# One step of a hybrid DeltaNet and attention backbone: the first norm with all shift and scale columns on TensorE, and smaller background pieces in DeltaNet

## The chip, the cores and the metric

The kernel runs on one core of a Trainium2 chip. The metric is the device time of one execution in microseconds, the median of several. TensorE does matrix products into PSUM, VectorE and ScalarE work element by element, GpSimd can do a few of VectorE's operations and cannot read PSUM, and SyncE (SP) issues all transfers between memory and the on-chip buffers. Each engine works through its own queue in order; semaphores hold an instruction back until its inputs are there.

## The reference

128 context tokens and 512 latent tokens, 640 together, go through one layer of width 2048. Everything is fp32.

```python
def ada_modulation(cond, w_ada, b_ada):
    m = jax.nn.silu(cond) @ w_ada + b_ada          # (B, 6 * D)
    return jnp.split(m[:, None, :], N_MOD, axis=-1)
...
    shift1, scale1, gate1, shift2, scale2, gate2 = ada_modulation(cond, p['w_ada'], p['b_ada'])
    h = modulate(rms_norm(x, p['norm1_g']), shift1, scale1)      # h * (1 + scale) + shift
    qkv, z, a, b, q_a, kv_a, k_pe = split_cols(h @ p['w_in'], IN_SPLITS)
    gdn_o, s_fin = gdn_mix(qkv, z, a, b, ...)      # silu(conv(qkv)), l2 norm, delta rule both ways, 8 heads
    ...                                            # 8 heads of latent attention, w_out, gated residual
    x = x + gate2 * conv_ffn(h2, p['w_up'], p['ffn_conv_w'], p['ffn_conv_b'], p['w_down'])
```

Context and latent tokens have a conditioning vector each (`c_ctx`, `c`), so every modulation column is made for two vectors. In DeltaNet each chunk needs the inverse of a unit triangular matrix.

## The kernel before, in words

**Number format.** A weight tile W is split into `whi`, a rounded copy in the type fp32r (ScalarE, line 129), and `wlo` = W - `whi` (VectorE, line 131). A dense product is then three fp32r products: whi·hi, whi·lo, wlo·hi. Activations carry the same split (`h_hi`, `h_lo`). Products in plain fp32 also occur, for small things; the profile shows each of them as two records.

**Dense products.** w_in is stored so that its columns come as z0 to z4, misc, then k, q, v of each head in turn, with the low-rank columns m and the last z between. `dense` (line 212 on) makes a pair of 128-column tiles from four weight chunks `kg`, each a load of 512 KB: 4 x 2 x 3 x 8 = 192 products of 320 columns. `w_next` keeps two raw chunks, and split chunks, ahead. Every 12 products `tick` advances the background generators, among them one per DeltaNet head.

**The first norm (lines 356 to 438).** x (16 tiles of 128 rows, `xs`) is loaded, squared on ScalarE and summed on VectorE (line 381, two buffers `sq`); `col_sums` puts the sum over rows on TensorE (line 244), and `rb` becomes 1/rms by Ln and Exp. The modulation columns come in units of 256. `ada` loads a unit's weights in four chunks of 512 KB (`araw`, a ring of three), splits each, and multiplies with the conditioning vectors as the four stationary columns (lines 264, 265: 32 products of 256 columns). ScalarE copies the 4 x 256 result out of PSUM (line 267), two small products turn it (line 272), VectorE adds the bias and the gain. `modulated` then makes v = x · scale · rb in four VectorE operations per unit (line 287), `h_hi` on ScalarE (line 289) and `h_lo` (line 290), for odd tiles on GpSimd. `part` does all that for one unit after the other. Eight units belong to scale1; with two of them done a quarter of the contraction of the first three tiles z0, z1, z2 can run. Six further units give 1536 of the 2048 shift columns beside the pair z3, z4. The last 512 shift columns come from `gemv_fill`, a background job on VectorE (line 326). The shift enters the later dense products as two extra columns of `h_hi` and `h_lo`.

**DeltaNet.** For each head, `sink` runs the convolution and the SiLU as soon as the dense tile is there, and spawns `gdn` and `gdn_q`. `gdn` solves the triangular blocks of both directions in one batch; one direction needs its blocks turned, which is a copy on ScalarE of 20 rows x 1024 with the two inner axes exchanged, on the way in (line 629) and on the way out (line 647). `neg` is minus the decay factor, for all heads at once. A `yield n` gives the engines to the dense stream for n ticks.

**Attention entry.** `kv_cache` and `key_rope` load the cached latents and rotary keys at the place in the program where they are split.

The order of the instructions on each engine is the order of a scheduler that goes by priorities from the program's order, so it is not exactly the order in the text.

Of the kernel before, what the change touches and what calls it, by code (L numbers as in the profile page):

```python
# [15 lines left out]
P = 128  # L16
# [29 lines left out]
NSP = 6  # L46
LA = 1
# [3 lines left out]
PK = ()  # L51
SH = 1.0
# [15 lines left out]
def step_kernel(ctx: ExitStack, tc: tile.TileContext, a, dbg=None, stop=None):  # L68
# [183 lines left out]
    def ada_load(c, kg, pl):  # L252
        raw = pl.tile([P, 4, 256], F32, tag="wraw", name="araw", bufs=3)
        sp.dma_start(raw, a["w_ada"][c, kg])
        return raw

    def ada(n, t0, cond, pl):

        ps = bank("ada_ps")
        for kg in range(4):  # L260
            hi, lo = split_chunk(ada_load(n, kg, pl), 256, pl, 3, (4 * n + kg) % 8 in PK)
            for k in range(4):
                kt = kg * 4 + k
                pe.matmul(ps[0:4, 0:256], cond[:, kt, :], hi[:, k, :], start=kt == 0, stop=False)
                pe.matmul(ps[0:4, 0:256], cond[:, kt, :], lo[:, k, :], start=False, stop=kt == 15)
# [3 lines left out]
        def last():  # L269
            ps2 = bank("ada_ps2")  # L270
            for j in range(2):
                pe.matmul(ps2[:, 2 * j:2 * j + 2], m4[:, j * P:(j + 1) * P], con[0:4, K_COMB:K_COMB + 2],
                          start=True, stop=True)
            dve.tensor_tensor(mod[:, t0:t0 + 2, :], ps2[:, 0:4].rearrange("p (j c) -> p j c", c=2),
                              v1(V_BADA + t0, 2).unsqueeze(2).broadcast_to([P, 2, 2]), ALU.add)
# [83 lines left out]
    h_hi = hp.tile([P, KT, T + 2], F32R, name="h_hi")  # L359
    h_lo = hp.tile([P, KT, T + 2], F32R, name="h_lo")  # L360
    zb = hp.tile([P, EZ, 2], F32, name="zb")

    def hmov(kt):
        return h_hi[:, kt, :], h_lo[:, kt, :]

    fill["ps"] = lambda: bank("ada_ps")
    with tc.tile_pool(name="xp", bufs=1, side="right") as xp:
        cond = xp.tile([P, KT, 4], F32R, name="cond")
        dve.tensor_copy(cond[:, :, 0:2], csil)
        dve.tensor_tensor(cond[:, :, 2:4], csil, cond.bitcast(F32)[:, :, 0:2], ALU.subtract)  # L370
        xs = xp.tile([P, KT, T], F32, name="xs")
        for c in range(8):
            sp.dma_start(xs[:, 2 * c:2 * c + 2, :], a["x"][:, 2 * c:2 * c + 2, :])
        acc = xp.tile([P, T], F32, name="acc1")
        for kt in range(KT):
            if kt == 0:
                act.activation(acc, xs[:, 0, :], AF.Square)
            else:
                sq = xp.tile([P, T], F32, tag="sq", name="sq", bufs=2)
                act.activation(sq, xs[:, kt, :], AF.Square)  # L380
                dve.tensor_tensor(acc, acc, sq, ALU.add)
        rb = xp.tile([P, T], F32, name="rb1")
        rstd_bcast(rb, col_sums(acc), 1.0 / D)

        def part(j):
            if j < 8:
                ada(j, 16 + 2 * j, cond, xp)()
                gain(16 + 2 * j, V_N1 + 2 * j, 2)
                for kt in (2 * j, 2 * j + 1):
                    v = xp.tile([P, T], F32, tag="sq", name="v", bufs=2)  # L390
                    modulated(xs, rb, h_hi, h_lo, kt, 16, v)

        def early(i, ps):

            zr = xp.tile([P, T], F32, tag="sq", name="zr", bufs=2)
# [22 lines left out]
        fill["step"] = SH  # L418
        fill["gen"] = gemv_fill([xp, 2, 1], ada_jobs(2 * NSP, 16))
        todo = list(range(NSP))  # L420
        last = []
        npair = (EZ - 3) // 2
        for p in range(1, 1 + npair):
            def shift(kg):
                n = 4 * (p - 1) + kg + 1
                while todo and (NSP - len(todo)) * 4 * npair < n * NSP:
                    c = todo.pop(0)
                    f = ada(8 + c, 2 * c, cond, xp)
                    if last:
                        last.pop()()  # L430
                    last.append(f)
                if last and n == 4 * npair:
                    last.pop()()
            dense(hmov, lambda i, ps: early(1 + 2 * p + i, ps), before=shift)
        for _ in fill["gen"]:
            pass
        dve.tensor_copy(h_hi[:, :, T:T + 2], mod[:, 0:KT, :])
        dve.tensor_tensor(h_lo[:, :, T:T + 2], mod[:, 0:KT, :], h_hi.bitcast(F32)[:, :, T:T + 2], ALU.subtract)
# [55 lines left out]
    neg = gp.tile([P, 5, 16], F32, name="neg")  # L494
# [3 lines left out]
    def gates(ps):  # L498
# [43 lines left out]
        dve.tensor_scalar(neg, eg, -1.0, None, ALU.mult)  # L542
# [4 lines left out]
    def gdn(h, st):  # L547
# [12 lines left out]
        gm = gmask(0)  # L560

# [19 lines left out]
        cc = gp.tile([P, 3, 2, 5], F32, name="cc", bufs=2)  # L581
        for d in range(2):
            dve.tensor_tensor(cc[:, 0, d, :], beta[:, :, 8 * d + h], rec, ALU.mult)
            dve.tensor_scalar(cc[:, 1, d, :], cc[:, 0, d, :], -1.0, None, ALU.mult)
            dve.tensor_tensor(cc[:, 2, d, :], cc[:, 0, d, :], edec[:, :, 8 * d + h], ALU.mult)

# [1355 lines left out]
```

## Time and profile before

| what | us |
|---|---|
| median of three runs | 3266.69 (3266.14 to 3268.99) |
| the profiled execution | 3265.16 |
| its span in the trace | 3263.4 |
| x being loaded and squared | 0 to 24 |
| tiles z0, z1, z2 with the first norm | 24 to 147 |
| tiles z3, z4 with the shift units | 147 to 206 |
| DeltaNet beside the other w_in columns | 206 to 990 |
| entry of the attention | 990 to 1045 |
| attention, w_out, FFN, last norm | 1045 to 3263 |

The stages are read from the first and last instructions of their lines. The span is the time between the first and the last instruction; 1.8 us of the execution lie around it. In the windows a busy time is a sum over the stretch, and PEclk is the share of full speed that TensorE was granted. In the waits a line says which instruction waited, for which engine's write to which tile, how long in all, how often, and the longest.

### The profile page before, as it was taken

The numbers are of one execution on the slowest core, as the hardware profiler recorded it, in microseconds if no ns is written. First come the engines' busy times: TensorE is split into PE (matmuls) and PEld (weight loads), VectorE is DVE, ScalarE is ACT, GpSimd is POOL, SyncE is SP. The second block draws the span as 40 slices with busy tenths as digits, with TensorE's granted clock in tenths as the row PEclk, the third lists the DMA queues.
The fourth block names the chain that finished last, engine by engine and source line by source line (L and its number), as shares of the span: only waits on it lengthen the run. The fifth ranks groups of instructions, "written<-read, shape, count | busy, mean of one in ns | idle before, by whom it ended". The sixth has DMA issues, their size and how long they took to land. (4 is left out here: it accounts for less than half of the span.)

```text
span 3263.4 us, 54513 instructions
## 1 busy us (share of the span) xinstructions
PE 3071.6 (94%) x21243; PEld 2972.8 (91%) x21243; DVE 2684.3 (82%) x4701; ACT 1453.0 (45%) x2245; POOL 334.3 (10%) x279
## 2 busy tenths in 40 slices
PE   5899999999998998997899999999999989999996
PEld 4689999999998998997899999999999989999995
DVE  7666666767567677998998898898898898999998
ACT  5434555555446543114544444444444454444433
POOL 1201000000000000003200000000010041111111
PEclk9899999999899999998999999999999999999998
DMA  7663222323224126883343333343343332333333
GB/s 271 201 198 86 72 78 67 117 68 100 74 87 135 45 81 236 270 263 121 127 136 97 110 128 108 111 131 110 98 140 102 95 125 94 113 98 110 110 116 121
DMA packets 181474, 403.92 MB, mean 124 GB/s; under 512 B 39392, under 2 KB 57952, under 8 KB 181216
## 3 DMA queue, kind: packets, MB, share of 16 engines
q1 hardware_dynamic: 181216, 400.44, 38.3%
q8 instruction: 167, 2.74, 0.4%
q14 instruction: 91, 0.75, 0.1%
HBM read 361.83 MB, written 38.54 MB: 123 GB/s over the span
## 5 line engine op out<-in xcount | busy, mean ns | idle before, releaser
L922 ACT CAST whi<-wraw 128x1024 fp32r<-128x1024 f32 x256 | 268.8, 1050 | 489.4 <-PE dn L198 202.8
L198 PE MATMUL mm<-b_hi,whi 128*128 128x320 f32 x1344 | 398.6, 310 | 4.2 <-ACT whi L922 3.9
L198 PE MATMUL mm<-b_lo,whi 128*128 128x320 f32 x1344 | 397.8, 310 | 0.0
L923 DVE TENSOR_TENSOR wlo<-wraw,whi 128x1024 fp32r<-128x1024 f32 x256 | 318.0, 1242 | 71.9 <-PE dn L207 62.9
L326 DVE SCALAR_TENSOR_TENSOR aacc<-araw,csil,aacc 128x512 f32<-128x512 f32 x510 | 369.0, 762 | 9.1 <-DMA araw<-in_w_ada_dram 8.7
L198 PE MATMUL mm<-h_lo,whi 128*128 128x320 f32 (+1 forms) x1312 | 318.7, 321 | 17.5 <-POOL h_lo L290 17.5
L198 PE MATMUL mm<-h_hi,whi 128*128 128x320 f32 (+1 forms) x1312 | 324.2, 327 | 7.5 <-ACT h_hi L289 4.8
L198 PE MATMUL dn<-b_hi,whi 128*128 128x320 f32 x1008 | 297.7, 309 | 0.0
L198 PE MATMUL dn<-b_lo,whi 128*128 128x320 f32 x1008 | 297.7, 309 | 0.0
L129 ACT CAST whi<-wraw 128x1024 fp32r<-128x1024 f32 (+1 forms) x138 | 143.0, 1036 | 327.3 <-PE mm L198 227.1
L198 PEld LDWEIGHTS mm<-b_hi,whi 128*128 128x128 f32 x1344 | 253.2, 188 | 5.0 <-ACT whi L922 4.4
L198 PEld LDWEIGHTS mm<-b_lo,whi 128*128 128x128 f32 x1344 | 253.2, 188 | 0.0
L198 PEld LDWEIGHTS mm<-h_lo,whi 128*128 128x128 f32 x1312 | 227.3, 194 | 21.5 <-POOL h_lo L290 19.6
L198 PEld LDWEIGHTS mm<-h_hi,whi 128*128 128x128 f32 x1312 | 227.2, 195 | 13.0 <-ACT h_hi L289 6.8
L1593 PE MATMUL mm<-b_hi,whi 128*128 128x320 f32 x672 | 204.6, 318 | 33.1 <-DVE x_lo L1600 9.4
L207 PE MATMUL mm<-h_hi,wlo 128*128 128x320 f32 (+1 forms) x1312 | 234.1, 318 | 0.0
L922 ACT CAST whi<-us 128x1024 fp32r<-128x1024 f32 (+1 forms) x126 | 123.4, 980 | 230.7 <-PE mm L198 160.3
L207 PE MATMUL mm<-b_hi,wlo 128*128 128x320 f32 x1344 | 224.4, 309 | 0.0
L131 DVE TENSOR_TENSOR wlo<-wraw,whi 128x1024 fp32r<-128x1024 f32 (+1 forms) x138 | 168.2, 1219 | 54.2 <-ACT whi L129 23.7
L207 PEld LDWEIGHTS mm<-h_hi,wlo 128*128 128x128 f32 x1312 | 202.8, 192 | 1.6
L207 PEld LDWEIGHTS mm<-b_hi,wlo 128*128 128x128 f32 x1344 | 204.0, 188 | 0.0
L1593 PE MATMUL mm<-b_lo,whi 128*128 128x320 f32 x672 | 202.2, 314 | 0.0
(534 smaller groups left out, 7461.2 us busy)
## 6 DMA issues: line engine op xcount, KB each, us to landing
wraw<-in_w_up_dram SPq DMA_DIRECT2D x176, 512.0 KB
araw<-in_w_ada_dram SPq DMA_DIRECT2D x272, 256.0 KB
wraw<-in_w_down_dram SPq DMA_DIRECT2D x88, 512.0 KB
wraw<-in_w_in_dram SPq DMA_DIRECT2D x80, 512.0 KB
araw<-in_w_ada_dram SPq DMA_DIRECT2D x56, 512.0 KB
wraw<-in_w_out_dram SPq DMA_DIRECT2D x32, 512.0 KB
graw<-g_d SPq DMA_DIRECT2D x44, 320.0 KB
g_d<-cg SPq DMA_DIRECT2D x44, 256.0 KB
```

The costliest lines, as they stand in the source:

```text
L129: act.copy(hi[:, :, 0:n], raw[:, :, 0:n])
L131: (pool if on_pool else dve).tensor_tensor(lo[:, :, 0:n], raw[:, :, 0:n], hi.bitcast(F32)[:, :, 0:n], ALU.subtract)
L198: pe.matmul(o, wts[0][:, k, col:col + P], m[:, sl], start=start and k + n == 0, stop=False)
L207: pe.matmul(o, wts[1][:, k, col:col + P], mov(k)[0][:, sl], start=False, stop=stop and k == 3)
L326: dve.scalar_tensor_tensor(acc[:, c, 0:w], raw, vecs[:, kt, c:c + 1], acc[:, c, 0:w], ALU.mult, ALU.add)
L922: act.copy(dst_hi, src)
L923: dve.tensor_tensor(dst_lo, src, dst_hi.bitcast(F32), ALU.subtract)
L1593: pe.matmul(dq[q], wt(w[0], k), bs[(2 * n + k) % 6][m][:, q, :], start=n == grp[0] and k + m == 0, stop=False)
```

## The change

First norm. The tiles of x now lie in the buffers that `h_hi` takes over later, two tiles to a buffer; with the room that this gives, the raw ring has eight chunks and the split buffers five. Every second square goes to TensorE as it is and is summed there. All 16 units of scale1 and shift1 go through `ada`; for the first eight the first chunk is multiplied unsplit in plain fp32. A unit's turn and all that follows is issued after the next unit's products. `h_lo` is always VectorE's. DeltaNet. The turning copies are cut in two with a step between. The SiLU of k, q and v moves from `sink` into the first step of a background generator. There is one more step before a head's last turn, and minus the decay factor is made per head. Attention entry. The cache loads are issued before the first projection.

```diff
-NSP = 6
-LA = 1
+NSP = 8
+AR = 8
+AH = 5
...
     def ada(n, t0, cond, pl):
         ps = bank("ada_ps")
         for kg in range(4):
-            hi, lo = split_chunk(ada_load(n, kg, pl), 256, pl, 3, (4 * n + kg) % 8 in PK)
+            raw = pl.tile([P, 4, 256], F32, tag="wraw", name="araw", bufs=AR)
+            sp.dma_start(raw, a["w_ada"][n, kg])
+            whole = n < 8 and kg == 0
+            movs = ((1, raw),) if whole else [(0, w) for w in split_chunk(raw, 256, pl, AH)]
             for k in range(4):
                 kt = kg * 4 + k
-                pe.matmul(ps[0:4, 0:256], cond[:, kt, :], hi[:, k, :], start=kt == 0, stop=False)
-                pe.matmul(ps[0:4, 0:256], cond[:, kt, :], lo[:, k, :], start=False, stop=kt == 15)
+                for m, (c, w) in enumerate(movs):
+                    pe.matmul(ps[0:4, 0:256], cond[c][:, kt, :], w[:, k, :], start=kt + m == 0,
+                              stop=kt == 15 and m == 1)
...
+            sq = acc if kt == 0 else xp.tile([P, T], F32, tag="sq", name="sq", bufs=4)
+            act.activation(sq, xs[kt // 2][:, kt % 2, 0:T], AF.Square)
+            if kt % 2:
+                for o, sl in tok_chunks(sums):
+                    pe.matmul(o, ones, sq[:, sl], start=kt == 1, stop=False)
+            elif kt:
                 dve.tensor_tensor(acc, acc, sq, ALU.add)
...
+        def ada_last():
+            if last:
+                n, f = last.pop()
+                f()
+                if n < 8:
+                    gain(16 + 2 * n, V_N1 + 2 * n, 2)
...
+                    for k, v in enumerate(vs_):
+                        act.copy(h_hi[n][:, k, 0:T], v)
+                        dve.tensor_tensor(h_lo[n][:, k, 0:T], v, h_hi[n].bitcast(F32)[:, k, 0:T], ALU.subtract)
...
+        def ada_next(count):
+            for _ in range(count):
...
+                f = ada(n, 16 + 2 * n if n < 8 else 2 * n - 16, (cond, condf), xp)
+                ada_last()
+                last.append((n, f))
...
-            for j in range(LA) if kg == 0 else ():
-                part(j)
-            for j in (2 * kg, 2 * kg + 1):
-                part(j + LA)
+            if kg == 0:
+                ada_next(1)
+                w_load(0)
+                w_load(1)
+            ada_next(3 if kg == 0 else 2)
...
-        fill["gen"] = gemv_fill([xp, 2, 1], ada_jobs(2 * NSP, 16))
...
-        act.copy(L[0:20], Lc[0:20].rearrange("p a b -> p b a"))
-        yield 1
+        for i in range(2):
+            act.copy(L[0:20, 16 * i:16 * i + 16, :], Lc[0:20, :, 16 * i:16 * i + 16].rearrange("p a b -> p b a"))
+            yield 1
...
+    def gdn_v(st, v):
+        act.activation(v, v, AF.Silu)
+        st["v"] = v
+        yield 1
...
             conv(ps, V_CW + off, 24, dst)
-            act.activation(dst, dst, AF.Silu)
```

In TensorE's queue, at the start of the second quarter of the contraction, before: `mm0`, `mm1`, `mm2` are the tiles z0 to z2, `ada_ps` the unit under way, and the dense products use the two tiles of x that the unit before it has just made:

```order
L265 MATMUL ada_ps_480<-wlo_499,cond_96 4x256
L264 MATMUL ada_ps_480<-whi_511,cond_96 4x256
L198 MATMUL mm0_161<-h_hi_90,whi_450 128x320 x2
L198 MATMUL mm1_162<-h_hi_90,whi_450 128x320 x2
L198 MATMUL mm2_163<-h_hi_90,whi_628 128x320 x2
L198 MATMUL mm0_161<-h_lo_91,whi_450 128x320 x2
L198 MATMUL mm1_162<-h_lo_91,whi_450 128x320 x2
L198 MATMUL mm2_163<-h_lo_91,whi_628 128x320
L198 MATMUL mm0_161<-h_hi_90,whi_450 128x320 x2
L198 MATMUL mm1_162<-h_hi_90,whi_450 128x320
L265 MATMUL ada_ps_480<-wlo_513,cond_96 4x256
```

and in the changed kernel, where `h_hi2`, `h_lo2` come from unit 2, and the two lines L271 are the turns of units 3 and 4:

```order
L271 MATMUL ada_ps_369<-con_73,m4_418 128x2 x2
L198 MATMUL mm0_177<-h_hi2_430,whi_496 128x320 x2
L198 MATMUL mm0_177<-h_lo2_431,whi_496 128x320
L271 MATMUL ada_ps_526<-con_73,m4_575 128x2 x2
L198 MATMUL mm0_177<-h_lo2_431,whi_496 128x320
L198 MATMUL mm0_177<-h_hi2_430,whi_496 128x320 x2
L198 MATMUL mm0_177<-h_lo2_431,whi_496 128x320
L264 MATMUL ada_ps_593<-araw_594,condf_103 4x256 x4
L264 MATMUL ada_ps_593<-whi_602,cond_102 4x256
L264 MATMUL ada_ps_593<-wlo_604,cond_102 4x256
L264 MATMUL ada_ps_593<-whi_602,cond_102 4x256
```

The dense products stood among the products of one unit, taking tile by tile; now the turns of units 3 and 4 stand close together, and all products of unit 5 lie between them and the first use of what unit 3 makes.

In VectorE's queue, for the first unit's two tiles, there is one difference `h_lo` before, the other being GpSimd's; `aacc` is the background job of shift columns:

```order
L274 TENSOR_TENSOR mod_78<-ada_ps2_223,vec_72 128x4
L131 TENSOR_TENSOR wlo_396<-wraw_392,whi_394 128x4x128
L282 SCALAR_TENSOR_TENSOR mod_78<-mod_78,vec_72 128x4
L287 SCALAR_TENSOR_TENSOR v_228<-xs_99,mod_78,rb1_155 128x512
L287 SCALAR_TENSOR_TENSOR v_228<-xs_99,mod_78,rb1_155 128x128
L287 SCALAR_TENSOR_TENSOR v_233<-xs_99,mod_78,rb1_155 128x512
L287 SCALAR_TENSOR_TENSOR v_233<-xs_99,mod_78,rb1_155 128x128
L131 TENSOR_TENSOR wlo_271<-araw_267,whi_269 128x1024
L290 TENSOR_TENSOR h_lo_91<-v_228,h_hi_90 128x640
L131 TENSOR_TENSOR wlo_285<-araw_281,whi_283 128x1024
L131 TENSOR_TENSOR wlo_317<-araw_313,whi_315 128x1024
L324 TENSOR_SCALAR aacc_1262<-araw_1258,csil_85 128x512 x2
```

and two in the changed kernel, with weight splits (`wlo`) of later units ahead of them:

```order
L273 TENSOR_TENSOR mod_78<-ada_ps_180,vec_72 128x4
L131 TENSOR_TENSOR wlo_246<-araw_242,whi_244 128x1024
L281 SCALAR_TENSOR_TENSOR mod_78<-mod_78,vec_72 128x4
L396 SCALAR_TENSOR_TENSOR v_290<-xs0_90,mod_78,rb1_174 128x512
L131 TENSOR_TENSOR wlo_260<-araw_256,whi_258 128x1024
L396 SCALAR_TENSOR_TENSOR v_290<-xs0_90,mod_78,rb1_174 128x128
L131 TENSOR_TENSOR wlo_274<-araw_270,whi_272 128x1024
L396 SCALAR_TENSOR_TENSOR v_291<-xs0_90,mod_78,rb1_174 128x512
L396 SCALAR_TENSOR_TENSOR v_291<-xs0_90,mod_78,rb1_174 128x128
L131 TENSOR_TENSOR wlo_313<-araw_309,whi_311 128x1024
L402 TENSOR_TENSOR h_lo0_297<-v_290,h_hi0_296 128x640
L402 TENSOR_TENSOR h_lo0_297<-v_291,h_hi0_296 128x640
```

Both differences of the unit moved into this queue, and four weight splits moved between its operations.

In ScalarE's queue in the second head's DeltaNet, before: the turning copy (L629), the PSUM read of the q tile (L478, L479), its convolution (L486), a table load and the SiLU (L871):

```order
L629 COPY L<-Lc 20x1024
L478 ACTIVATE raw_1817<-mm_2907,b 128x512
L479 ACTIVATE raw_1817<-mm_2907,b 128x128
L486 ACTIVATE kq<-raw_1817,vec 128x641
L129 CAST whi<-wraw 128x1024
L871 ACT_TABLE_LOAD
L871 ACTIVATE kq<-kq 128x641
L478 ACTIVATE raw_1821<-mm_2908,b 128x512
L827 ACTIVATE q_3342<-kq 128x641
```

and in the changed kernel, where L645 is the copy in halves and L852 the SiLU:

```order
L645 COPY L<-Lc 20x512 x2
L742 ACTIVATE U<-v_ps,cc 128x128
L492 ACTIVATE raw_1834<-mm_2839,b 128x512
L742 ACTIVATE U<-v_ps,cc 128x128
L493 ACTIVATE raw_1834<-mm_2839,b 128x128
L500 ACTIVATE kq<-raw_1834,vec 128x641
L129 CAST whi<-wraw 128x1024
L852 ACT_TABLE_LOAD
L852 ACTIVATE kq<-kq 128x641
L492 ACTIVATE raw_1838<-mm_2840,b 128x512
L854 ACTIVATE q_3341<-kq 128x641
```

Two scalings of another head's result (L742) moved in behind the halves; the SiLU stands where it stood.

## Rows read from the trace of the kernel before

**Rows 1.** The page's line of engines: busy us, share of the span, instructions.

```profile
PE 3071.6 (94%) x21243; PEld 2972.8 (91%) x21243; DVE 2684.3 (82%) x4701; ACT 1453.0 (45%) x2245; POOL 334.3 (10%) x279
```

**Rows 2.** Windows by stage: length, busy us (instructions) per engine, clock, DMA share, GB/s.

```profile
0.00:24.00 24.00, 0.00 (x1) 0.00 (x1) 12.87 (x19) 14.27 (x20) 0.20 (x4) 1.00 0.86 329
24.00:147.00 123.00, 95.91 (x581) 76.10 (x582) 94.98 (x124) 60.97 (x74) 30.97 (x8) 0.89 0.65 209
147.00:206.00 59.00, 57.03 (x422) 47.55 (x420) 36.79 (x40) 29.60 (x34) 0.00 (x0) 1.00 0.72 237
206.00:990.00 784.00, 758.64 (x5740) 725.32 (x5739) 529.39 (x1405) 386.40 (x760) 44.40 (x44) 0.95 0.30 90
990.00:1045.00 55.00, 44.73 (x266) 42.19 (x267) 45.76 (x70) 39.59 (x64) 0.00 (x0) 0.91 0.43 140
```

**Rows 3.** Waits of TensorE from 24 to 147 us: total us, times, longest.

```profile
PE mm L198 <- POOL h_lo L290: 17.5, 7, 4.3
PE mm L198 <- ACT h_hi L289: 4.8, 6, 1.8
```

**Rows 4.** Groups of instructions, 24 to 147 us: busy us, mean ns | idle before.

```profile
L131 DVE TENSOR_TENSOR wlo<-araw,whi 128x1024 fp32r<-128x1024 f32 x35 | 43.5, 1276 | 3.0 <-ACT whi L129 2.9
...
L290 POOL TENSOR_TENSOR h_lo<-v,h_hi 128x640 fp32r<-128x640 f32 x8 | 31.0, 3871 | 108.1 <-ACT h_hi L289 108.1
...
L287 DVE SCALAR_TENSOR_TENSOR v<-xs,mod,rb 128x512 f32<-128x512 f32 (+1 forms) x32 | 15.5, 546 | 0.2
...
L290 DVE TENSOR_TENSOR h_lo<-v,h_hi 128x640 fp32r<-128x640 f32 x8 | 6.5, 818 | 0.0
```

**Rows 5.** Timeline of TensorE at four places: start us, length us, instruction.

```profile
28.19 0.28 PE L264 MATMUL ada_ps<-whi,cond 128*4 128x256 f32 x1
...
29.32 0.28 PE L264 MATMUL ada_ps<-whi,cond 128*4 128x256 f32 x1
...
44.24 0.60 PE L272 MATMUL ada_ps<-con,m 4*128 4x2 f32 x4
44.77 0.28 PE L264 MATMUL ada_ps<-whi,cond 128*4 128x256 f32 x1
...
930.20 1.34 PE L207 MATMUL mm<-h_hi,wlo 128*128 128x320 f32 x8
...
933.78 1.34 PE L207 MATMUL mm<-h_hi,wlo 128*128 128x320 f32 x8
...
975.60 0.60 PE L739 MATMUL qs_ps<-Sh,kq 128*128 128x256 f32 x2
976.04 0.61 PE L736 MATMUL o_ps<-U,IT 128*128 128x128 f32 x4
```

**Rows 6.** Timeline, first and last square, then the sums over rows.

```profile
8.69 0.74 ACT L377 ACTIVATE acc<-xs 128x640 f32<-128x640 f32 x1 [4.84 <-DMA xs<-in_x_dram]
...
22.12 0.74 ACT L380 ACTIVATE sq<-xs 128x640 f32<-128x640 f32 x1 [0.19 <-DVE acc L381]
...
24.00 2.50 PE L244 MATMUL mm<-acc,con 128*128 128x320 f32 x4 [24.00 <-DVE acc L381]
```

**Rows 7.** Waits of TensorE from 206 to 990 us.

```profile
PE g_ps L607 <- ACT vp L740: 6.7, 3, 2.2
PE ot_ps L816 <- DVE vp L798: 3.2, 4, 1.5
...
PE mm L198 <- ACT raw L479: 2.5, 3, 1.0
```

**Rows 8.** Groups of instructions on ScalarE, 206 to 990 us.

```profile
L871 ACT ACT_TABLE_LOAD x16 | 20.5, 1283 | 0.3
...
L629 ACT COPY L<-Lc 20x1024 f32<-20x1024 f32 x8 | 16.8, 2103 | 2.0 <-DMA Lc<-l_d 2.0
```

**Rows 9.** The longest wait of TensorE from 990 to 1045 us.

```profile
PE pj L188 <- ACT rsrc L1007: 4.5, 1, 4.5
```

**Rows 10.** Timeline of ScalarE near 1012 us.

```profile
1011.71 1.28 ACT L922 CAST qh<-mm 128x640 fp32r<-128x640 f32 x2
```

More of the change, by code (lines that the diff above doesn't have):

```diff
@@ L357, in step_kernel @@
     hp = hst.enter_context(tc.tile_pool(name="hp", bufs=1))
-    h_hi = hp.tile([P, KT, T + 2], F32R, name="h_hi")
-    h_lo = hp.tile([P, KT, T + 2], F32R, name="h_lo")
+    xs = [hp.tile([P, 2, HW], F32, name=f"xs{j}", tag=f"h_hi{j}") for j in range(8)]
+    h_hi, h_lo = [], []
     zb = hp.tile([P, EZ, 2], F32, name="zb")
     def hmov(kt):
-        return h_hi[:, kt, :], h_lo[:, kt, :]
+        return h_hi[kt // 2][:, kt % 2, :], h_lo[kt // 2][:, kt % 2, :]
     fill["ps"] = lambda: bank("ada_ps")
@@ L374, in step_kernel @@
         acc = xp.tile([P, T], F32, name="acc1")
+        sums = ps_pair(0)
         for kt in range(KT):
[L376 to L380, printed above, removed]
+            sq = acc if kt == 0 else xp.tile([P, T], F32, tag="sq", name="sq", bufs=4)
[4 more added lines that the diff above has]
+            elif kt:
@@ L381, in step_kernel @@
                 dve.tensor_tensor(acc, acc, sq, ALU.add)
+        for o, sl in tok_chunks(sums):
+            pe.matmul(o, ones, acc[:, sl], start=False, stop=True)
         rb = xp.tile([P, T], F32, name="rb1")
[L383 to L391, printed above, removed]
+        rstd_bcast(rb, sums[:, C0:C0 + T], 1.0 / D)
@@ L424, in shift @@
             def shift(kg):
[L425 to L433, printed above, removed]
+                if p < npair:
+                    return
+                if kg < 3:
+                    ada_next(2)
+                else:
+                    ada_last()
             dense(hmov, lambda i, ps: early(1 + 2 * p + i, ps), before=shift)
[L435 to L438, printed above, removed]
     fst = ctx.enter_context(ExitStack())
@@ L580, in gdn @@
         dve.reciprocal(rec, ss)
-        cc = gp.tile([P, 3, 2, 5], F32, name="cc", bufs=2)
+        cc = gp.tile([P, 4, 2, 5], F32, name="cc", bufs=2)
         for d in range(2):
@@ L646, in gdn @@
         Xp = gp.tile([40, 32, 32], F32, name="Xp", tag="cmp")
-        act.copy(Xp[0:20], L[0:20].rearrange("p a b -> p b a"))
+        sp.dma_start(x_d[20:40], L[20:40])
+        for i in range(2):
+            act.copy(Xp[0:20, 16 * i:16 * i + 16, :], L[0:20, :, 16 * i:16 * i + 16].rearrange("p a b -> p b a"))
+            if i == 0:
+                yield 1
         sp.dma_start(x_d[0:20], Xp[0:20])
-        sp.dma_start(x_d[20:40], L[20:40])
         for q in range(4):
@@ L799, in gdn @@
         st["normed"] = True
+        if h < H - 1:
+            yield 1
         if h < EZ:
@@ L1063, in proj @@
                 p_rope(w, q2 // 2, i)
+                if q2 == 0 and i == 0:
+                    kv_cache()
                 yield
```

67 lines of the change are left out of this document (34 added, 33 removed).

## The prediction

> **What bounds the kernel now.** I read the page's engine line first: TensorE is busy 94% of the span [rows 1], so time can only come from stretches where it stands still, is given the half clock, or does work that can go. The windows then cut the program at its stages [rows 2]. In the first 24 us TensorE does nothing. From 24 to 147 us, where the first three column tiles are made while x is normed, it is busy 95.9 of 123 us at a mean granted clock of 0.89. From 147 to 206 us (tiles z3 and z4 beside the shift units) it is busy 57.0 of 59 at 1.00. In the DeltaNet stretch it is busy 758.6 of 784 at 0.95, and where DeltaNet passes into attention 44.7 of 55 at 0.91. After 1045 us nothing is edited, and from inside the attention on the engines issue the same instructions in the same order as before, so I cost that part at nothing.
>
> The stretch from 24 to 147 us is the worst, and its loss splits in two. Idle time is 123 - 95.9 = 27.1 us. A mean clock of 0.89 between the levels 1.2 and 2.4 GHz means that 22% of the stretch, 27 us, ran at half speed, which costs another 13.5 us. The waits name the cause of the idle part [rows 3]: 17.5 us in seven waits on `h_lo` written by GpSimd, 4.8 on `h_hi`. The reason is in the groups [rows 4]: the same subtraction takes 3.87 us on GpSimd and 0.82 on VectorE.
>
> **The first norm, step by step.** TensorE's prices are start-to-start times at full clock [rows 5]: a dense product of 320 columns is (933.78 - 930.20) / 24 = 0.149 us; a modulation product of 256 columns in the split format (29.32 - 28.19) / 10 = 0.113; one of 256 columns in plain fp32 976.04 - 975.60 = 0.44; the turn of one unit's result (L272) 44.77 - 44.24 = 0.53.
> - Work before in 24 to 147: 288 dense x 0.149 = 42.9, eight units x 32 x 0.113 = 28.9, eight turns 4.2, the column sums 2.5 (24.00 to 26.50, [rows 6]); together 78.5. With the idle 27.1 and the clock's 13.5 that is 119, so about 4 us are gaps between instructions that the three prices miss. I keep those 4.
> - Added: the last 512 shift columns come over from VectorE's background sums as two more units, and the first norm's stretch now holds ten: 2 x (32 x 0.113 + 0.53) = 8.3. Eight units take their first quarter in plain fp32: 32 products of 0.44 in place of 64 of 0.113, +6.8. Removed from here: the 2.5 of sums, which move ahead of it.
> - So the work is 78.5 + 4 + 8.3 + 6.8 - 2.5 = 95.1 us: more than before, and the change has to win that back.
> - The start. Squares come every 0.93 us before, since each waits for VectorE's add: 8.69 to 22.86, then sums from 24.0 to 26.5 [rows 6]. In the new order eight squares go straight to TensorE (16 fp32 products of 320 columns) and VectorE adds seven. Held by nothing but ScalarE, 16 squares of about 0.72 us end near 20.2; the last four products, 0.55 each by columns from the 0.44, bring the sums to 22.4. TensorE starts the units there.
> - The remaining loss. h_lo of all 16 tiles is now VectorE's (0.82 us), and a unit's turn is issued behind the next unit's products, so its copy off PSUM no longer stops TensorE. Two things are late next. The weights: one unit is four loads of 512 KB, 6.4 us at the 329 GB/s of the first window [rows 2]; x is in at about 17.6, so units 0 and 1 are in at 24.0 and 32.8 (with 0.8 MB of w_in between), and TensorE, with 4.5 us of work per unit, stands about 4 us. Then each later quarter of the contraction waits for its second unit's chain (turn 0.53, four products v of 0.55 and a difference of 0.82 [rows 4], a cast and small operations: some 5 us, an estimate) behind one unit's 3.2 to 4.5 us of products: about 1 us, three times. I take 7 us idle. For the clock I take 3 us, a quarter of before, since it fell beside those waits. Bounds of both together: 0 (every wait hidden) and 40.6 (all as before).
> - This part ends at 22.4 + 95.1 + 10 = 127.5, where it ended at 147. VectorE has room: 95.0 us busy there before [rows 2]; it loses 32 background sums and eight adds and gains eight differences of 0.82.
> - The second part is 57.0 of 59 us TensorE already [rows 2]. Its units are still six; it loses the final sums of the background job and gains two turns of 0.53, and the ring of eight raw buffers fills ahead. I take 57.5. The next stage then starts at 185, not 206: **-21 us**, with -31.5 at no loss and +10 at the whole old loss.
>
> **DeltaNet.** TensorE's idle time is 25.4 us in 784. Of it the extra step before the head's last turn meets 3.2 us in four waits (`ot_ps` on `vp`), and shorter blocks on ScalarE meet 2.5 us in three waits of dense products on the PSUM read `raw` [rows 7]. The turning copies take 2.1 us each, two per head [rows 8]; in halves each blocks ScalarE for about 1.05. What two starts cost more than one is hidden, since ScalarE is 49% busy there [rows 2]. The SiLUs keep nearly their place in ScalarE's queue, as the order shows. They are no longer grouped at one point, though: the stage has 61 table loads for 57, 4 x 1.28 = 5.1 us of ScalarE [rows 8]. `neg` per head is two tiny VectorE ops, hidden in its 32% idle. I take 4 of the 5.7 us of waits: **-4**. Bounds: -12 if the three waits of `g_ps` (6.7, [rows 7]) go too, +8 if the table loads and the later steps land on TensorE's path (5.1 plus two or three steps of about 1 us).
>
> Here a rule speaks against the edit. The rows show a table load of 1.283 us with the next instruction right behind it [rows 8]. The Trainium skill ("ScalarE: Activation LUTs", What ACT_TABLE_LOAD costs) counts 2.66 us per switch, drain included, and (Table sets: the hidden batching unit) asks that calls be batched by table set, which SiLU steps among Exp and Ln undo. By the page the four loads would be 10.6 us of ScalarE, by the row 5.1; the sum goes by the row.
>
> **Attention entry.** The order puts the loads of the cache ahead of the next weight load on SP. They are needed by ScalarE, not directly by TensorE, whose one long wait there is 4.5 us for the copy `rsrc` [rows 9]. In the new order ScalarE makes that copy ahead of two casts of 1.28 us together [rows 10]. **-1**; bounds 0 and -4.5.
>
> **Sum.** -21 - 4 - 1 = -26 against the profiled execution's 3265.2 gives 3239; the median of the runs shown is 1.5 above it, so I predict 3240.
>
> **Rivals.**
> 1. *The wait changes its name.* h_lo now stands in VectorE's queue behind weight splits of 1.28 us [rows 4], and the casts to h_hi stand behind weight casts on ScalarE. For it: in-order queues, VectorE 77% busy [rows 2]. Against: split buffers go from three to five, so splits run ahead. If 24 of the 40.6 us of loss stay, the stage gains 7, with DeltaNet 3: 3257.
> 2. *The SiLU steps cost.* Stage -21, DeltaNet +8: 3253. For it: the four more table loads, at head starts where ScalarE is fullest. Against: ScalarE is half idle on the whole. The rule on table sets above makes this one; the trace bears out its direction, not its size.
> 3. *More than I take.* Loss of only 2 us in the first part and the full -12 in DeltaNet, whose 0.95 clock alone is worth 39 us: -29 - 12 - 2 = -43, 3224.
> 4. *Slower.* TensorE gets 15.1 us more products in the first part. If nothing of the 40.6 us goes, because the wait for each quarter is really the wait for its second unit whichever engine writes it, the stage ends 10 us later and DeltaNet gives nothing: 3276. It decides from a loss of 31 us in that part upward, where the stage gains nothing.
> That transfers bound it I leave out: the first three windows moved 24 x 329 + 123 x 209 + 59 x 237 = 47.6 MB [rows 2], 145 us at 329 GB/s, well before 185.
>
> **How the numbers follow.** Forecast 0.52 (its own range 3230 to 3250), rival 1 0.16, rival 2 0.13, rival 3 0.15, rival 4 0.04. The range 3220 to 3258 leaves out rival 4, the upper half of rival 1 and the lower edge of rival 3. A change under 0.2% (6.5 us) can't be told from none here: faster is all of the forecast, rivals 2 and 3 and most of rival 1, 0.91; same 0.05; slower 0.04.
>
> **What would show it.** The first dense product with the shift columns near 185 us, not 206; no wait on a GpSimd h_lo; the clock above 0.95 between 24 and 128; `ot_ps` gone from the waits; the DeltaNet stretch between 775 and 784 us. The forecast is wrong if the first three tiles end later than 138 us (rival 1), if DeltaNet grows (rival 2), or if either is below 120 or 772 (rival 3).

## The result, and the profile after

The changed kernel takes 3223.7 us (median of four runs, 3223.0 to 3229.7) against 3267.6 for the kernel before, run beside it (four runs, 3266.1 to 3269.0): ratio 0.987, 95% interval 0.9853 to 0.9887, 44 us less. The forecast was 3240, with 3224 as its third rival. The profiled execution has a span of 3221.2 us, 42.2 less than before.

The page's line of engines after, to set beside [rows 1]:

```profile
PE 3073.4 (95%) x21331; PEld 2969.1 (92%) x21331; DVE 2659.8 (83%) x4692; ACT 1462.0 (45%) x2275; POOL 311.4 (10%) x272
```

TensorE is busy as long as before in a shorter span, although it got more products: busy time shrinks where the clock rises. The windows after, by stage, with columns as in [rows 2]; DeltaNet is cut here at the last PSUM read of z4 and of the last w_in tile (182.2 and 954.2 us):

```profile
0.00:24.00 24.00, 13.80 (x40) 8.08 (x41) 7.21 (x12) 14.44 (x20) 0.35 (x5) 1.00 0.94 350
24.00:127.00 103.00, 98.14 (x644) 73.22 (x641) 79.18 (x113) 61.47 (x80) 0.00 (x0) 0.95 0.80 288
127.00:182.00 55.00, 55.00 (x412) 47.75 (x412) 28.25 (x37) 26.75 (x38) 0.00 (x0) 1.00 0.50 175
182.00:954.00 772.00, 746.01 (x5754) 715.81 (x5753) 542.79 (x1428) 402.84 (x790) 52.14 (x44) 0.97 0.31 93
954.00:998.00 44.00, 40.47 (x246) 37.76 (x245) 38.20 (x59) 33.20 (x55) 0.00 (x0) 0.92 0.44 139
```

The kernel before at the same two events (204.9 and 996.1 us):

```profile
205.00:996.00 791.00, 761.62 (x5757) 728.03 (x5757) 536.39 (x1414) 392.16 (x768) 44.40 (x44) 0.95 0.30 91
996.00:1040.00 44.00, 37.75 (x231) 36.23 (x230) 35.59 (x54) 31.92 (x54) 0.00 (x0) 0.91 0.46 145
```

So z4 is done 22.7 us earlier (204.9 to 182.2), DeltaNet is 19.2 us shorter (791.2 to 772.0), the attention's first head is stored 4.4 us sooner after the last w_in tile (75.1 us for 79.5), and 4.1 us are lost again behind that: 22.7 + 19.2 + 4.4 - 4.1 = 42.2.

One reading is used throughout. A stretch's length is work at full clock, plus TensorE's idle time, plus what half-clock stretches cost: the sum over windows of 2 us, the last one cut at the stretch's end, of (1 - granted clock) x length, worked out from some 390 windows (the two digits of a long window's clock leave 4 us open). For DeltaNet that is 722.9 + 29.4 + 38.9 = 791.2 before and 723.8 + 26.0 + 22.2 = 772.0 after. The work is the same within 1 us, the idle time fell by 3.4; 16.7 of the 19.2 us are clock. From 22 us to the end of z2 (147.1 before, 126.9 after), work rose from 82.4 to 94.9, idle time fell from 29.1 to 4.9 and the clock's cost from 13.7 to 5.1.

TensorE's waits after, from 24 to 127 us, where [rows 3] had 17.5 us on `h_lo` and 4.8 on `h_hi`, and the group that answers to [rows 4]:

```profile
PE ada_ps L264 <- DVE wlo L131: 4.1, 4, 1.3
PE ada_ps L264 <- ACT whi L129: 0.7, 1, 0.7
```

```profile
L402 DVE TENSOR_TENSOR h_lo<-v,h_hi 128x640 fp32r<-128x640 f32 x16 | 12.5, 819 | 2.4 <-ACT h_hi L401 2.4
```

Both waits are on weight splits, none on what is made from x. In DeltaNet the waits after, beside [rows 7], are:

```profile
PE v_ps L733 <- ACT vp L724: 6.6, 4, 2.3
PE ab_ps L520 <- ACT ab L492: 3.0, 1, 3.0
PE q_ps L860 <- ACT q L854: 2.6, 3, 0.9
PE mm L198 <- ACT raw L493: 2.1, 3, 0.9
```

`g_ps` (6.7 us) is gone, and `v_ps` (2.4 before) took its place with 6.6. `ot_ps` kept 1.8 us in three waits, and the waits on `raw` 2.1 of 2.5. What the halves did to ScalarE is in its groups, to set beside [rows 8], and then in its timeline:

```profile
L645 ACT COPY L<-Lc 20x512 f32<-20x512 f32 x16 | 17.5, 1138 | 3.0 <-DMA Lc<-l_d 3.0
```

```profile
254.10 2.23 ACT L645 COPY L<-Lc 20x512 f32<-20x512 f32 x2
256.35 1.28 ACT L852 ACT_TABLE_LOAD   x1
```

All 16 pairs stand like this one: two halves in one row, nothing between, 2.13 to 2.23 us a pair where the whole copy took 2.04 to 2.14. The step between the halves changed when later instructions come, but not how long ScalarE is blocked.

### The profile page after: what moved, and what is told of

It is laid out like the page before. It is cut to its first block, busy times and chain, and to the rows that moved or that the text cites. A ratio compares the mean times of both kernels' runs of the same rounds, so it can differ in the third digit from the quotient of the medians.

```text
span 3221.2 us, 54708 instructions
## 1 busy us (share of the span) xinstructions
PE 3073.4 (95%) x21331; PEld 2969.1 (92%) x21331; DVE 2659.8 (83%) x4692; ACT 1462.0 (45%) x2275; POOL 311.4 (10%) x272
## 5 line engine op out<-in xcount | busy, mean ns | idle before, releaser
L317 DVE SCALAR_TENSOR_TENSOR aacc<-araw,csil,aacc 128x512 f32<-128x512 f32 x480 | 345.3, 757 | 9.2 <-DMA araw<-in_w_ada_dram 8.7
L198 PE MATMUL mm<-h_lo,whi 128*128 128x320 f32 (+1 forms) x1312 | 311.9, 316 | 0.0
```

The source lines that it names most:

```text
L198: pe.matmul(o, wts[0][:, k, col:col + P], m[:, sl], start=start and k + n == 0, stop=False)
L317: dve.scalar_tensor_tensor(acc[:, c, 0:w], raw, vecs[:, kt, c:c + 1], acc[:, c, 0:w], ALU.mult, ALU.add)
```

## The experiments

Below, theory A says that DeltaNet's clock loss belongs to the order of its instructions, theory B that it differs from one execution to the next. Length, work, idle and clock loss of DeltaNet come from the one profiled execution of each kernel; the median is over its runs.

| kernel | z4 done | DeltaNet | work | idle | clock | profiled run | median (runs, span of times) |
|---|---|---|---|---|---|---|---|
| before | 204.9 | 791.2 | 722.9 | 29.4 | 38.9 | 3265.2 | 3267.6 (4, 3266 to 3269) |
| changed | 182.2 | 772.0 | 723.8 | 26.0 | 22.2 | 3223.0 | 3223.7 (4, 3223 to 3230) |
| e1 first norm only | 182.2 | 796.5 | 721.5 | 32.1 | 42.9 | 3249.9 | 3248.9 (4, 3245 to 3250) |
| e2 DeltaNet only | 207.2 | 783.9 | 722.8 | 20.2 | 41.0 | 3259.9 | 3254.5 (9, 3240 to 3261) |
| e3 cache loads only | 199.1 | 789.9 | 723.4 | 31.0 | 35.5 | 3261.2 | 3263.1 (10, 3259 to 3272) |
| e4 h_lo on GpSimd | 183.1 | 775.2 | 723.3 | 28.0 | 23.9 | 3227.4 | 3228.0 (4, 3226 to 3229) |
| e5 SiLU back | 181.3 | 791.5 | 722.2 | 30.0 | 39.3 | 3240.5 | 3226.7 (4, 3224 to 3241) |
| e6 copies whole | 178.9 | 798.3 | 722.3 | 30.5 | 45.5 | 3249.3 | 3245.2 (5, 3234 to 3249) |
| e7 no extra step | 182.3 | 775.0 | 719.5 | 31.0 | 24.5 | 3230.3 | 3232.0 (4, 3227 to 3234) |
| e8 shifted by 5.1 | 187.3 | 781.6 | 720.1 | 22.2 | 39.2 | 3236.4 | 3231.6 (4, 3224 to 3236) |
| e9 whole, with steps | 179.9 | 779.3 | 726.3 | 22.2 | 30.7 | 3227.3 | 3231.2 (5, 3227 to 3242) |
| e10 turn at once | 184.7 | 780.6 | 721.2 | 23.6 | 35.8 | 3232.5 | 3228.1 (5, 3221 to 3234) |
| e11 rings of three | 187.8 | 773.9 | 724.1 | 27.6 | 22.2 | 3230.9 | 3235.4 (6, 3231 to 3243) |
| e12 root on VectorE | 181.4 | 767.2 | 722.9 | 24.6 | 19.7 | 3221.0 | 3221.2 (5, 3217 to 3232) |

For e8 the 5.1 us of added products are counted with the time before DeltaNet. Beside these experiments the kernel before ran 37 times, 3249.8 to 3271.5, medians 3264.4 to 3268.3. With such spreads a difference of 3 us between two of these kernels is not told apart. The stages spread as well. Up to z4 eight kernels (changed, e1, e5 to e9, e12) have one order of instructions and finish it at 178.9 to 182.3 us, and three (before, e2, e3) have the order of before and finish it at 199.1 to 207.2.

**e1, the first norm's edits alone.**

The first norm whole, of which the constants stand here, and `neg` per head, whose room it needs:

```diff
-NSP = 6
-LA = 1
+NSP = 8
+AR = 8
+AH = 5
...
-    neg = gp.tile([P, 5, 16], F32, name="neg")
...
```

> The kernel before with the first norm's edits alone (and minus the decay factor per head, whose room the norm's buffers need); the DeltaNet steps, the turning copies and the cache loads are as before. Theory A (the DeltaNet edits themselves removed the half-clock stretches): the stage ends near 183 us as in the changed kernel, DeltaNet keeps its 792 us and its 39 us of half-clock time lost, total -23 us, near 3244. Theory B (where the half clock falls is a matter of how the bursts of small products happen to lie, and any shift changes it): the stage ends near 183, but DeltaNet differs from 792 by 8 us or more without any edit in it; total between 3220 and 3255.

Median 3248.9, ratio 0.9938 (0.9922 to 0.9955). The first stage is the changed kernel's, and DeltaNet went back to long:

```profile
24.00:127.00 103.00, 98.16 (x645) 73.47 (x643) 79.47 (x113) 61.76 (x80) 0.00 (x0) 0.95 0.78 289
...
182.00:979.00 797.00, 764.92 (x5745) 729.34 (x5745) 537.76 (x1427) 392.74 (x770) 44.50 (x44) 0.95 0.29 90
```

The norm's 22.7 us are its own, and the other 19 of the changed kernel come with the other edits. Theory A has this run: DeltaNet is within 8 us of its old length, with its clock loss.

**e2, the DeltaNet edits alone** (the halves shown, and the SiLU steps, the extra step and `neg`).

```diff
-        act.copy(L[0:20], Lc[0:20].rearrange("p a b -> p b a"))
-        yield 1
+        for i in range(2):
+            act.copy(L[0:20, 16 * i:16 * i + 16, :], Lc[0:20, :, 16 * i:16 * i + 16].rearrange("p a b -> p b a"))
+            yield 1
...
```

> The kernel before with the DeltaNet edits alone (SiLU in background steps, turning copies in halves, the extra step before a head's last turn, minus the decay factor per head). Theory A: first norm ends at 206 us as before, DeltaNet loses 14 to 19 of its 792 us, nearly all of it half-clock time, total near 3250. Theory B: DeltaNet changes by any amount between -19 and +8; the idle time of TensorE there stays near 26 to 29 us either way. The prediction's own price was -4: near 3263.

Median 3254.5, ratio 0.9953 (0.9937 to 0.9968), but the runs lie between 3240 and 3261. The profiled one (3259.9) is near the upper end: its idle time fell by 9 us (29.4 to 20.2), its clock loss did not fall (38.9 to 41.0). Neither theory's number fits: the same instructions give runs 21 us apart.

**e3, the cache loads alone** (with the split of the cache one step later, as in the changed kernel).

```diff
+    cck = lend("qh", 512, "cck").rearrange("p (k c) -> p k c", k=4)
+    sp.dma_start(cck, a["cache_ckv"])
+    kr = lend("kh", 768, "kr")[0:64]
...
     def kv_cache():
-        cck = lend("qh", 512, "cck").rearrange("p (k c) -> p k c", k=4)
-        sp.dma_start(cck, a["cache_ckv"])
```

> The kernel before with the cache loads issued early and the split of the cache one step later, nothing else. If this edit made the attention entry shorter (47 to 42 us from the last w_in tile on), the entry shrinks by 4 to 5 us here too and the total is near 3262. If the entry got shorter because the last head of DeltaNet ended earlier, the entry stays within 1 us and the total at 3267.

Ratio 0.9996 (0.9981 to 1.001): no difference. From the last w_in tile to the store of the attention's first head it took 81.6 us, against 79.5 before and 75.1 changed; e2, without these loads, took 74.2. The entry got shorter by DeltaNet's edits, not by the loads.

**e4, h_lo of the odd tiles back on GpSimd.**

```diff
-                        dve.tensor_tensor(h_lo[n][:, k, 0:T], v, h_hi[n].bitcast(F32)[:, k, 0:T], ALU.subtract)
+                        (pool if k % 2 else dve).tensor_tensor(h_lo[n][:, k, 0:T], v, h_hi[n].bitcast(F32)[:, k, 0:T], ALU.subtract)
```

> The changed kernel with h_lo of the odd tiles back on GpSimd. If GpSimd's 3.9 us per tile was what held TensorE in the first norm, the stage ends 10 to 20 us later than 183 and waits on a GpSimd h_lo of 10 us or more are back. If the pipelined turn (a unit's turn behind the next unit's products) and the deeper rings did it, the later h_lo is hidden: stage end within 4 us of 183, waits on h_lo under 4 us.

z4 is done at 183.1, 0.9 us later than in the changed kernel and close to the 178.9 to 182.3 of the changed order, and TensorE waits 1.2 us for GpSimd. But the price changed as well. GpSimd's group and one of its rows in this kernel:

```profile
L402 POOL TENSOR_TENSOR h_lo<-v,h_hi 128x640 fp32r<-128x640 f32 x8 | 13.1, 1632 | 107.3 <-ACT h_hi L401 97.0 <-DVE h_lo L402 6.2 <-DVE wlo L131 4.1
```

```profile
59.67 1.33 POOL L402 TENSOR_TENSOR h_lo<-v,h_hi 128x640 fp32r<-128x640 f32 x1 [6.80 <-ACT h_hi L401]
```

and one of GpSimd in the kernel before, with VectorE beside it:

```profile
120.45 6.16 POOL L290 TENSOR_TENSOR h_lo<-v,h_hi 128x640 fp32r<-128x640 f32 x1 [9.20 <-ACT h_hi L289]
...
123.62 0.68 DVE L131 TENSOR_TENSOR wlo<-wraw,whi 128x512 fp32r<-128x512 f32 x1
124.22 1.21 DVE L131 TENSOR_TENSOR wlo<-araw,whi 128x1024 fp32r<-128x1024 f32 x1
125.36 1.80 DVE L326 SCALAR_TENSOR_TENSOR aacc<-araw,csil,aacc 128x512 f32<-128x512 f32 x1
```

The same subtraction takes 1.33 us where VectorE leaves room and 6.16 beside a VectorE that runs operations with two tensor inputs back to back; the VectorE row at 125.36 took 1.80 us where that line's 76 rows average 0.76 from 206 us on, so each held up the other. The Trainium skill ("SBUF — State Buffer", SBUF: two separate sides) says that the two engines share a pair of ports, that a VectorE operation with two SBUF inputs or a GpSimd operation that reads SBUF takes it whole, and that the other waits; these rows agree. So 3.87 us [rows 4] was the price of GpSimd beside that VectorE queue, and this run shows that `h_lo`'s engine hardly matters any more, not that it did not matter before.

**e5, SiLU back in its old place.**

```diff
             conv(ps, V_CW + off, 24, dst)
+            act.activation(dst, dst, AF.Silu)
...
-                spawn(gdn_v(st, dst))
+                st["v"] = dst
```

> The changed kernel with the SiLU of k, q and v back where the dense tile is taken out of PSUM, everything else as changed. If the SiLU steps removed the half-clock time of DeltaNet, its clock loss goes from 22 back to about 40 us and the total to about 3242. If they cost table loads, as the second rival of the prediction had it, DeltaNet gets shorter by 2 to 8 us, total 3216 to 3222. If the clock loss hangs on where bursts happen to lie (theory B), it changes by 5 us or more in either direction with idle time as it was.

Median 3226.7 for 3223.7: not told apart. The profiled run took 3240.5, with 39.3 us of clock loss; the other three took 3224 to 3228 at a granted clock of 0.972 to 0.976. The SiLU steps neither gave nor cost anything that shows. The table loads of the second rival this run can't price, since they did not go: between z4 and the last w_in tile ScalarE loads a table 68 times here, 67 in the changed kernel and 63 in the one before.

**e6, whole turning copies and their old steps** (the copy out likewise).

```diff
-        for i in range(2):
-            act.copy(L[0:20, 16 * i:16 * i + 16, :], Lc[0:20, :, 16 * i:16 * i + 16].rearrange("p a b -> p b a"))
-            yield 1
+        act.copy(L[0:20], Lc[0:20].rearrange("p a b -> p b a"))
+        yield 1
...
```

> The changed kernel with the turning copies whole again (2.1 us each instead of two of about 1 us). By the prediction's own price the waits that the halves removed come back: 2 to 4 us of TensorE's idle time in DeltaNet, total 3226 to 3228. If the halves removed the half-clock time, the clock loss goes from 22 to about 40, total about 3242.

Median 3245.2, ratio 0.994 (0.992 to 0.996), all five runs above all four of the changed kernel: 21 us, by far the most of any single edit taken back. Idle time rose by 4.5 us, clock loss by 23.3. The old wait is back:

```profile
PE g_ps L622 <- ACT vp L755: 5.7, 4, 2.2
```

**e7, without the step before the head's last turn.**

```diff
         st["normed"] = True
-        if h < H - 1:
-            yield 1
```

> The changed kernel without the extra step before a head's last turn. By the prediction's price the four waits of the turn on vp come back, +3 us, total 3227. If the step is what moved the bursts of small products away from the half clock, the clock loss goes from 22 to about 40, total about 3242.

Median 3232.0, four runs of 3227 to 3234. That is 8.3 us above the changed kernel, where the price was 3. The waits of the turn came back with more than was priced (1.8 us to 7.5), idle time rose from 26.0 to 31.0, the clock loss by only 2.3:

```profile
PE ot_ps L835 <- DVE vp L817: 7.5, 6, 2.1
```

**e8, the changed kernel shifted.**

```diff
             dense(hmov, lambda i, ps: early(1 + 2 * p + i, ps), before=shift)
+        dly = bank("dly")
+        for _ in range(34):
+            pe.matmul(dly[:, 0:320], h_hi[0][:, 0, 0:P], h_hi[0][:, 0, 0:320], start=True, stop=True)
```

> The changed kernel with 34 more dense products of 320 columns (34 x 0.149 = 5.1 us) ahead of DeltaNet, their result unused; nothing in DeltaNet is edited. Theory A (the clock loss belongs to the order of DeltaNet's instructions): DeltaNet keeps 772 us with a clock loss of 22, total +5 = 3229. Theory B (it belongs to when the stretches happen to fall): the clock loss changes by 8 us or more, total outside 3224 to 3234.

Runs of 3223.7, 3231.5, 3231.6 and 3236.4 at granted clocks of 0.975, 0.971, 0.974 and 0.969. But for a few rows at its start DeltaNet has the changed kernel's order of instructions, on TensorE from 235 us on without a difference; its clock loss in the profiled run is 39.2 us for 22.2. The triangular solve of the seventh head shows it best, the same 172 instructions on TensorE; first the changed kernel, then this one:

```profile
817.80:828.90 11.10, 11.10 (x172) 9.64 (x171) 5.63 (x12) 5.75 (x16) 1.20 (x1) 1.00 0.16 51
```

```profile
832.10:845.80 13.70, 13.70 (x172) 11.95 (x171) 6.67 (x15) 7.48 (x23) 2.26 (x2) 0.78 0.11 40
```

11.1 us at full clock, 13.7 at a mean of 0.78, with TensorE busy throughout in both. What the clock does in the solve is not fixed by the order: the clock loss is theory B's, though the median of 3231.6 lies within 3 us of theory A's total. The Trainium skill ("TensorE: Matmul & The Clock Gate", Part 1: The HAM clock gate) says that the chip watches TensorE's activity on a grid of its own that does not start anew with a kernel; the spread between executions of one order agrees, but no run here shows the grid.

**e9, whole copies with the halves' steps.**

```diff
-        for i in range(2):
-            act.copy(L[0:20, 16 * i:16 * i + 16, :], Lc[0:20, :, 16 * i:16 * i + 16].rearrange("p a b -> p b a"))
-            yield 1
+        act.copy(L[0:20], Lc[0:20].rearrange("p a b -> p b a"))
+        yield 2
...
+        yield 1
+        act.copy(Xp[0:20], L[0:20].rearrange("p a b -> p b a"))
```

> The changed kernel with whole turning copies (2.1 us each), but with the same steps between the parts of a head as the halves have (two after the copy in, one before the copy out). In the changed kernel's trace the two halves of all 16 copies run back to back, 2.13 to 2.23 us a pair against 2.04 to 2.14 for a whole one before, so ScalarE is blocked as long as it was. If the gain of the halves (3245 without, 3224 with) comes from the steps that they brought, this kernel is at 3221 to 3231. If it comes from the shorter single copy, as the prediction priced it, it is at 3240 to 3250.

Median 3231.2, at the upper edge of what the steps would give (3221 to 3231), runs of 3227 to 3242. No wait of `g_ps` on `vp` is left. Of the 21.5 us between e6 and the changed kernel 14 are the steps', together with the earlier store of the rows that are not turned (`x_d[20:40]`), which e9 keeps and e6 takes back; the other 7.5 may be scatter.

**e10, each unit turned at once.**

```diff
-                ada_last()
                 last.append((n, f))
+                ada_last()
```

> The changed kernel with each modulation unit's turn and all that follows issued right behind its own products instead of behind the next unit's. If the later turn is what removed TensorE's idle time in the first norm (27.1 us before, 4.9 now, and h_lo on GpSimd gave back under 1 us), idle time there rises by 12 us or more with 4 us or more of half-clock loss, the stage ends at 198 or later, total near 3240. If the rings of eight and five did it, the stage ends within 4 us of 183.

z4 is done at 184.7, 2.5 us later; TensorE's waits there are short, with one of 2.1 on `h_hi`. Taken back alone, the later turn does not bring the idle time back (5.6 us up to z2 for 4.9). DeltaNet has the changed kernel's order again, and 35.8 us of clock loss.

**e11, rings of three.**

```diff
-AR = 8
-AH = 5
+AR = 3
+AH = 3
```

> The changed kernel with three raw chunks and three split buffers in the first norm as before, instead of eight and five. If the rings removed the idle time, 12 us or more of it come back and the stage ends at 195 or later, total near 3236. If the later turn did it, the stage ends within 4 us of 183, total 3222 to 3229. By the prediction's own account (the weights are late only for units 0 and 1) it is the second.

z4 is done at 187.8, 5.6 us later, between the two numbers expected. The waits from 24 to 188 us are now on the casts:

```profile
PE ada_ps L264 <- ACT whi L129: 7.3, 5, 3.2
PE ada_ps L264 <- DVE wlo L131: 2.1, 4, 1.0
```

A quarter of the 22.7 us is the rings', as waits for weights. DeltaNet, the same order once more, lost 22.2 us to the clock.

**e12, k's root on VectorE.**

```diff
-        act.activation(lnk, ss, AF.Ln)
-        act.activation(rki, lnk, AF.Exp, scale=0.5)
+        dve.tensor_scalar(rki, ss, 1 / 13.7, 3.43, ALU.mult, ALU.add)
+        for _ in range(3):
+            dve.reciprocal(lnk, rki)
+            dve.scalar_tensor_tensor(lnk, lnk, 0.5, ss, ALU.mult, ALU.mult)
+            dve.scalar_tensor_tensor(rki, rki, 0.5, lnk, ALU.mult, ALU.add)
```

> The changed kernel with the square root of k's norm made by ten small VectorE operations (a start value and three Heron steps, enough for sums between 12 and 180; these are 14 to 160 here) in place of Ln and Exp on ScalarE: 14 fewer table loads. Before, three waits of g_ps on vp (6.7 us) stood behind two table loads of this root, and now four waits of v_ps on vp (6.6 us). If the wait only changed its name, it goes here, with the half-clock stretches that follow some of these waits: DeltaNet 6 to 12 us shorter, total 3211 to 3218. If another wait takes its place again, total within 4 us of 3224.

Median 3221.2, runs of 3217 to 3232, ratio 0.9867 (0.985 to 0.9885): not told apart from the changed kernel. The long `v_ps` waits on `vp` are gone, others grew, here behind the last w_in tile:

```profile
PE pj L188 <- ACT rsrc L1037: 3.8, 1, 3.8
PE mm L188 <- DVE ql L952: 2.5, 1, 2.5
```

DeltaNet is 4.8 us shorter, but from the last w_in tile to the first head's store it takes 79.9 us for 75.1: all of it is given back. That is with 53 table loads for 67, so fourteen loads fewer, with VectorE operations in their place, do not show in the time.

## Why the forecast was right in sign and short in size

**First norm: -21 forecast, -22.7 measured, with the cause not settled.** The terms hold: work 95.1 forecast and 94.9 measured (1.2 of it the last sums: the units start at 23.2, forecast at 22.4), loss 10 and 10.0 (4.9 idle, 5.1 clock), end at 127.5 and 126.9; the second part took 55.3 for 57.5. That 10 us of loss came out to the tenth is luck: in the same order e6 and e9 lost 1.7 us to the clock there. The cause was named as `h_lo` on GpSimd plus the turn at once. Taken back one at a time, `h_lo`'s engine gives back 0.9 us, the turn 2.5, the rings 5.6, together 9 of 22.7, against 3.4 us of spread in one order. So no single one of them carries the stage; whether two of them cover for each other is not shown, since no run takes back two at once, `h_lo`'s engine and the turn least of all, which the forecast named together. e10 shows why the turn is hardly needed: there unit 7's `h_lo` is done at 109.1 us and the last quarter of the products starts at 117.9, since one more unit stands ahead of each quarter than before. That lead, the background sums that left VectorE, and the first quarter unsplit were not taken back alone; how the remaining 14 us divide stays open.

**DeltaNet: -4 forecast, -19.2 measured; this term was mis-sized.** Its step was "in halves each blocks ScalarE for about 1.05", and that failed: the halves run back to back. The waits that it took off (`ot_ps`, the reads of `raw`) moved by 1.8 us. The idle time fell by 3.4 in all, close to the 4 forecast, but partly by luck: half of it came from other waits, and the five kernels of the changed order have between 22.2 and 28.0 us of idle time. The forecast counted the steps that the halves brought only as a possible cost; by e9 most of what e6 gives back is theirs. The rest is clock, which the forecast gave no term; only the third rival noted that it was worth 39 us.

Two things stand behind the clock. The first is seen in the trace of before: a wait of 2.2 us on `g_ps`, with its cause on ScalarE (two table loads of the root of k's norm ahead of the copy `vp`), and the clock behind it:

```profile
337.74 1.28 ACT L578 ACT_TABLE_LOAD   x1
...
339.52 1.28 ACT L579 ACT_TABLE_LOAD   x1
340.81 0.21 ACT L579 ACTIVATE sm<-sm 128x5 f32<-128x5 f32 x1
340.92 0.25 ACT L740 COPY vp<-o_ps 128x128 f32<-128x128 f32 x1
```

```profile
339.00:341.30 2.30, 0.08 (x1) 0.08 (x1) 0.35 (x1) 2.23 (x7) 2.30 (x2) 1.00 0.10 29
341.30:344.80 3.50, 3.50 (x17) 3.50 (x18) 1.59 (x7) 1.21 (x5) 0.10 (x1) 0.51 0.00 0
344.80:347.00 2.20, 2.20 (x16) 2.20 (x16) 2.20 (x8) 0.00 (x0) 0.00 (x0) 1.00 0.00 0
```

TensorE stands for 2.2 us and then runs 3.5 us at 1.2 GHz (0.51): the wait costs 2.2 + 1.7 = 3.9 us. All three of these waits before were followed by such a stretch, at 341, 430 and 518 us. They are gone wherever the new steps stand (changed, e9) and back where they do not (e1, e6). In this pair of executions that is 6.7 + 3 x 1.7 = 11.8 us. `v_ps` took 4.2 of it back as idle time (6.6 for 2.4), but none of its four waits was followed by a half-clock stretch. That a stretch follows is not fixed either: of the `g_ps` waits on `vp` two of three were followed by one in e3, three of four in e1 and one of four in e6, and in e9 a `v_ps` wait was. The same wait in e3, in the order of before, with full clock behind it:

```profile
333.50:335.80 2.30, 0.06 (x2) 0.04 (x1) 0.35 (x1) 2.23 (x7) 2.30 (x2) 1.00 0.10 29
335.80:339.30 3.50, 3.50 (x27) 3.50 (x28) 2.34 (x10) 1.25 (x5) 0.12 (x1) 1.00 0.00 0
```

So these waits explain little of the 23.3 us of clock that e6 lost.

The second is the triangular solve, where the clock falls in some heads and not in others: two of eight in the profiled changed run. The changed order of DeltaNet ran in five kernels (changed, e4, e8, e10, e11), with clock losses of 22.2, 23.9, 39.2, 35.8 and 22.2 us, mean 28.7; the order of before ran in two (before, e3), with 38.9 and 35.5, mean 37.2. Theory B holds for this part, and half of the 16.7 us of clock between the two profiled runs was luck: the means differ by 8.5. Less the delay of its first stage each of the five has a median of 3223.7, 3227.1, 3226.5, 3225.6 and 3229.8, mean 3226.5; e1 has 3248.9. So on the new first norm DeltaNet's edits, with the entry, are worth about 22 us over many runs, and theory A holds for that. On the old one they are worth 12.5 (e2, 3254.5, against the median of 3267.0 of before beside it), so the two parts do not simply add up; why stays open. Which property of the order makes the fall in a solve rarer stays open: the number of dense products inside one does not sort the heads (in all five kernels the clock fell in the first head's solve with 21 of them and never in the second's with 23).

**Attention entry: -1 forecast, -4.4 measured, for another reason.** The loads do nothing (e3). The last head of DeltaNet ends earlier against the dense stream: its store comes 4.8 us after the last w_in tile's read instead of 9.3, in e2 as well.

**After 1045 us: nothing forecast, +4.1 measured.** On TensorE, VectorE and ScalarE the order is the same from 1239.2 us before and 1193.9 after on (a gain of 45.2). From there to the end 3.1 us are lost again, and the clock's cost there is 50.6 us for 47.9.

**The rivals.** The wait did change its name (`g_ps` to `v_ps`), but not in the stage where the first rival had it. The second fell: DeltaNet did not grow, and fourteen table loads fewer do not show (e12). The third had the time, 3224, with less gain in the first part and more in DeltaNet than it put there. The fourth fell. Of the forecast's signs, the start of the next stage near 185 us (182.2) and the end of the waits on GpSimd came true; the clock from 24 to 128 us was 0.95 and not above it, `ot_ps` kept 1.8 us of waits, and DeltaNet with 772.0 us was shorter than its 775 to 784.

## What to carry to other kernels

Price a wait of TensorE with the half-clock stretch that may follow it, here 2.2 us of idle time and 1.7 us of clock (after 9 of the 14 `g_ps` waits on `vp` in four traces), and read length as work + idle + clock before arguing from idle time alone. A cut only shortens a block if something stands between the pieces: look in the order for the two halves in one row. And repeat a profile, or run the same order in several kernels, before a few heads' clock is put down to an edit.

## What the runs showed of the hardware

- e3 has the order of before up to the attention's entry, and yet z4 was done 5.8 us sooner: 8.5 us of clock loss up to z2 for 13.7, and 26.2 us idle for 29.1.
- A wait of 2.2 us on TensorE was followed by 3.5 us at 1.2 GHz in one execution and by full clock in another of the same order (before at 341 us, e3 at 336 us).
- One kernel's times spread by 3 to 21 us, in step with the mean granted clock: 3223.7 at 0.975 and 3236.4 at 0.969 for e8. The same 172 TensorE instructions took 11.1 us at full clock and 13.7 at a mean of 0.78, with no idle time in either.
- One GpSimd subtraction of 128 x 640 takes 1.32 to 6.16 us, by what VectorE runs beside it.
